# A hybrid decoder layer: weights split into high and low parts by whole loaded tiles instead of halves

## The chip, the core and the metric

The kernel runs on one core of a Trainium2 chip. The core has engines with instruction streams of their own: TensorE (PE, matrix products; its weight loads are listed as PEld), VectorE (DVE), ScalarE (ACT), GpSimd (POOL) and SyncE (SP), which issues most of the transfers. They wait for each other by semaphores. The metric is the device time of one execution in microseconds; a profile is one such execution, recorded instruction by instruction.

## What is computed

One layer over 256 tokens of width 2048, batch 1, all in float32. Cut to its skeleton, with the shapes written behind:

```
u    = rms_norm(x, norm1_g)                  # 256 x 2048
proj = u @ w_in                              # 2048 x 6432
q, k, v, z = split(proj)                     # 3 x 1024 columns, and 3360 for z
attn = dilated_attention(q, k, v, bias)      # 16 heads of 64, three dilation patterns
rw   = rwkv7_time_mix(z, ...)                # 16 heads of 64, a recurrence over the tokens
h    = x + concatenate(attn, rw) @ w_out     # 2048 x 2048
u    = rms_norm(h, norm2_g)
gate, up = split(u @ w_gate_up)              # 2048 x 11264
h    = h + (silu(gate) * up) @ w_down        # 5632 x 2048
return rms_norm(h, final_g)
```

Both sides of every large product are float32. The kernel writes a weight w as a sum of two parts in the matmul's own rounded float32 type (F32R): high, a rounded copy of w, and low, w minus that copy. The activation is split likewise. A product is then three matmuls: high times high, high activation times low weight, low activation times high weight.

## The kernel before

**The weights' way.** All large weights pass one pipeline, in the order of a list `plan`: first the 288 low-rank columns of z (called `lo`), then per half of the heads the columns of r, k, v (z) and of v, q, k (attention), then w_out, then gate and up in turn for 11 groups of 512 hidden columns, then w_down in four slabs of 512 output columns. An entry of `plan` is one load: 1024 columns of float32 on 128 partitions, which are two chunks (kc) of 128 rows by 512 columns, or four chunks of 128 by 256, or in `lo` two of 128 by 288. The stages:

- `load` (L121 on): SP issues a DMA (L126) from the weight into a raw tile `wr`. There are RAWB = 3 raw tiles.
- `make` (L134 to L151): for each half j of the raw tile ACT copies it into `wh` (L148, the rounded high part), and DVE subtracts that copy from the raw tile into `wl` (L149, the low part). A half is one chunk of 512 or two of 256. There are SPLB = 6 buffers of 512 columns for wh and as many for wl.
- `take` (L158 to L166): hands one chunk to a consumer, and calls `make` ahead, so that in the program's order some 6 chunks (AHEAD), that is three tiles, are split ahead of the one in use.
- consumers: `slab` (L169, six matmuls per chunk of 512, L178 to L180), `slab_T` (L183, chunks of 256, L191 to L193), `slab_2T` (L1062, eight matmuls per chunk for gate and up, L1068 and L1069).

The last 8 chunks of w_down (KEEP) are split into four tiles that stay, since each is read twice.

**What sets the order.** Beside the large products runs side work: the attention and the recurrence. Each piece of it is a generator, and `run` and `step` (L201 to L233) put steps of these generators between the chunks of the main products. The program text made so is then arranged by a scheduler into one fixed order for each engine. So a split stands in ACT's and DVE's rows between other work of these engines: a row that waits holds up what stands behind it. A raw tile is free for the next load when its last subtract is done; a wh or wl buffer is free when PE's last matmul on it is done.

**Names in the rows.** `u1h` is the high part of x transposed (made from `pt_u` by ACT, L252), `lo` the product of it with the 288 columns, `zlo` its scaled copy (L413, L416), which PE transposes (`ptlo`). `zkh`, `zrh`, `zvh` are products for one half of the heads, `z_zvh` and `zv_h` the steps that finish the last of these (L476, L344). `bsh` is a sum over heads made by two matmuls of `bhh` and `blh` (L553 to L557). `kp_h`, `y_h`, `mix`, `bk_h` are the recurrence's arrays on DVE. In the recurrence `Zh` is a product with the state `Sh` (L803), DVE adds it into `av_h` (L806), and PE turns that into `Xh` (L811). `p` and `o` are the products with w_out (`part`), `ga`, `gb`, `up` gate and up, `d` down.

Of the kernel before, what the change touches and what calls it, by code (L numbers as in the profile page):

```python
# [10 lines left out]
F32 = mybir.dt.float32  # L11
F32R = mybir.dt.float32r
AF = mybir.ActivationFunctionType
ALU = mybir.AluOpType
AX = mybir.AxisListType

P = 128
# [58 lines left out]
def layer(ctx: ExitStack, tc: tile.TileContext, I, out, dbg=None, upto=99):  # L76
    nc = tc.nc
    PE, ACT, DVE, POOL, SP = nc.tensor, nc.scalar, nc.vector, nc.gpsimd, nc.sync
# [6 lines left out]
    wp = ctx.enter_context(tc.tile_pool(name="wp", bufs=1))  # L85
# [31 lines left out]
    plan, made, wq = [], {}, [0, 0]  # L117
# [12 lines left out]
    def ahead(n):  # L130
        while len(raws) < min(n, len(plan)):
            load(len(raws))

    def make(i):  # L134
        w_ap, kcs, col, n, keep = plan[i]
        ahead(i + 1)
        raw = raws[i]
        g = 2 if n == 256 else 1
        for j in range(2):
            if keep:  # L140
                both = keep.pop(0)
                hi, lo = both[:, 0, :], both[:, 1, :]
            else:
                hi = wp.tile([P, 512], F32R, tag="whi", name=f"wh{i}_{j}", bufs=SPLB)
                lo = wp.tile([P, 512], F32R, tag="wlo", name=f"wl{i}_{j}", bufs=SPLB)
            hi, lo = (a.rearrange("p (g n) -> p g n", g=g) for a in (hi, lo))
            src = raw[:, j * g:(j + 1) * g, :n]
            ACT.activation(hi[:, :, :n], src, AF.Copy)  # L148
            DVE.tensor_tensor(lo[:, :, :n], src, hi[:, :, :n].bitcast(F32), op=ALU.subtract)  # L149
            for k in range(g):  # L150
                made[(w_ap.tensor.name, kcs[j * g + k], col)] = (hi[:, k, :], lo[:, k, :])  # L151

    def plan_slab(w_ap, kcs, col, n, keep=None):
        g = 4 if n == 256 else 2
# [3 lines left out]
    def take(w_ap, kc, col, units=1):  # L158
        key = (w_ap.tensor.name, kc, col)
        while wq[0] < len(plan) and (key not in made or wq[0] * 2 < wq[1] + AHEAD):  # L160
            make(wq[0])
            wq[0] += 1
        wq[1] += units
        return made.pop(key)
# [151 lines left out]
    for half in range(2):  # L316
        for blks in ((4, 3, 5), (2, 0, 1)):
            for blk in blks:
                col = blk * AW + half * 512
# [16 lines left out]
    keep = []  # L336
# [689 lines left out]
    fp = ctx.enter_context(tc.tile_pool(name="fp", bufs=1, reuse_waits="tile"))  # L1026
# [5 lines left out]
    u2 = [fp.tile([P, 4, 2, SEQ], F32R, tag=f"u2{g}", name=f"u2{g}") for g in range(4)]  # L1032
# [74 lines left out]
        POOL.dma_start(t, I["final_g"].rearrange("(o d) -> o d", o=1)[:, i * 1024:(i + 1) * 1024].broadcast_to([P, 1024]))  # L1107
    fg = lambda sl: fgs[sl // 2][:, sl % 2 * 512:sl % 2 * 512 + 512]
    for g in range(4):
        kt = fp.tile([P, 2, 2, 512], F32R, tag=f"u2{g}", name=f"kept{g}")  # L1110
        keep += [kt[:, 0], kt[:, 1]]
    outr = out.rearrange("o (t p) d -> p (o t) d", p=P)
    hlhs = pair(hid_h, hid_l)

# [41 lines left out]
        print("SBUF free", tile.free_sbuf_bytes_per_partition(tc))  # L1156


RAWB, SPLB, AHEAD = 3, 6, 6
KEEP = 8  # L1160
LAT = (6, 5, 2, 6, 5, 3)
BS = 1.0
# [28 lines left out]
```

## Time and profile before

| | |
|---|---|
| median of 3 runs | 1232.54 us (1231.67 to 1233.33) |
| the profiled execution | 1232.04 us, of it 1230.3 us are its span |
| PE busy | 1214.8 us |
| DVE busy | 818.4 us |
| ACT busy | 698.7 us |
| bytes moved by DMA | 224.05 MB |

How such rows are read. In a list of groups a row has the line, the engine, the operation, what is written and read with their shapes, the count, the busy time in us and the mean of one in ns, and behind the last bar how long the engine was idle just ahead of them, and what ended that. In a timeline a row has the start and the length in us; "x3" behind it means that three such instructions follow each other and are drawn as one, and the square bracket has the idle time ahead and what ended it. A list of waits has total, count and longest. The roughly 1.7 us between span and time lie outside the recorded instructions.

### The profile page before, as it was taken

The page shows a single profiled execution, that of the slowest core. Times are in us where ns is not written, and L with a number is a line of the kernel's source. Part 1 is how long each engine was busy: PE and PEld are TensorE (multiplying, and loading weights), DVE is VectorE, ACT ScalarE, POOL GpSimd, SP SyncE. Part 2 cuts the span into 40 slices and gives each one's busy share as a digit, 9 for nine tenths or more (in the row PEclk, how much of TensorE's full clock was granted, in tenths as well). Part 3 has the DMA queues.
Part 4 walks back from the last instruction along what each step waited for, and adds up shares of the span by engine and source line. Part 5 has one row for each costly group of instructions (what it writes and reads, how often), then busy time and mean ns, then how long its engine had stood idle before and what let it go on. Part 6 is the DMA issues. An engine that isn't in the chain of part 4 may idle for free.

```text
span 1230.3 us, 21227 instructions
## 1 busy us (share of the span) xinstructions
PE 1214.8 (99%) x7932; PEld 1061.2 (86%) x7932; DVE 818.4 (67%) x1561; ACT 698.7 (57%) x1328; POOL 39.5 (3%) x64
## 2 busy tenths in 40 slices
PE   8999999999999999999999999999999999999997
PEld 7998999898997788888888888888888888888885
DVE  5887786698787467666666666566566655555653
ACT  7874546584556556655555555555565555454443
POOL 4000000001000000000000000000000000010100
PEclk9999999999999999999999999999999999999999
DMA  8656566356566257666666666666666666666663
GB/s 249 201 160 193 154 178 173 85 151 178 168 192 183 86 167 227 189 199 193 189 189 189 189 190 188 191 189 193 193 188 193 189 189 190 199 192 194 184 202 139
DMA packets 148472, 224.05 MB, mean 182 GB/s; under 512 B 18396, under 2 KB 65760, under 8 KB 148368
## 3 DMA queue, kind: packets, MB, share of 16 engines
q1 hardware_dynamic: 132176, 211.12, 58.3%
q10 hardware_dynamic: 13920, 6.06, 1.9%
q0 software_dynamic: 2272, 5.50, 1.4%
q8 instruction: 62, 1.02, 0.4%
q14 instruction: 42, 0.34, 0.1%
HBM read 218.96 MB, written 3.69 MB: 181 GB/s over the span
## 4 chain that ended last, share of the span: by engine, by line
PE 93%; DVE 2%; DMA 2%; ACT 1%; issue 1%; SPq 0%; POOLq 0%; POOL 0%; ACTq 0%; DVEq 0%
PE up L1068 13%; PE gb L1068 7%; PE ga L1068 7%; PE up L1069 7%; PE d L179 6%; PE d L178 6%; PE d L180 6%; PE gb L1069 3%; PE ga L1069 3%; PE o L178 2%; PE o L180 2%; PE o L179 2%; PE kTb L191 1%; PE qTb L191 1%; PE kTb L192 1%; PE kTb L193 1%
## 5 line engine op out<-in xcount | busy, mean ns | idle before, releaser
L149 DVE TENSOR_TENSOR wl<-wr,wh 128x512 fp32r<-128x512 f32 (+1 forms) x792 | 541.7, 691 | 338.4 <-ACT wh L148 321.1
L148 ACT ACTIVATE wh<-wr 128x512 fp32r<-128x512 f32 (+1 forms) x792 | 493.3, 627 | 466.3 <-DVE wl L149 234.8
L1068 PE MATMUL up<-u,wh 128*128 128x512 f32 x704 | 244.6, 394 | 0.0
L1069 PE MATMUL up<-u,wl 128*128 128x256 f32 x704 | 195.0, 277 | 0.0
L1068 PEld LDWEIGHTS up<-u,wh 128*128 128x128 f32 x704 | 132.0, 188 | 30.7
L1069 PEld LDWEIGHTS up<-u,wl 128*128 128x128 f32 x704 | 132.1, 188 | 0.0
L178 PE MATMUL d<-wh,hh 128*128 128x512 f32 x336 | 130.7, 389 | 0.0
L180 PE MATMUL d<-wh,hl 128*128 128x512 f32 x336 | 130.7, 389 | 0.0
L179 PE MATMUL d<-wl,hh 128*128 128x512 f32 x336 | 130.7, 389 | 0.0
L1068 PE MATMUL gb<-u,wh 128*128 128x512 f32 x352 | 130.2, 394 | 0.0
L1068 PE MATMUL ga<-u,wh 128*128 128x512 f32 x352 | 130.0, 394 | 0.0
L1069 PE MATMUL ga<-u,wl 128*128 128x256 f32 x352 | 97.5, 277 | 0.0
L1069 PE MATMUL gb<-u,wl 128*128 128x256 f32 x352 | 97.5, 277 | 0.0
L1068 PEld LDWEIGHTS ga<-u,wh 128*128 128x128 f32 x352 | 66.0, 188 | 15.3
L1068 PEld LDWEIGHTS gb<-u,wh 128*128 128x128 f32 x352 | 66.0, 188 | 15.2
L178 PEld LDWEIGHTS d<-wh,hh 128*128 128x128 f32 x336 | 63.1, 188 | 13.2
L180 PEld LDWEIGHTS d<-wh,hl 128*128 128x128 f32 x336 | 63.1, 188 | 13.1
L179 PEld LDWEIGHTS d<-wl,hh 128*128 128x128 f32 x336 | 63.1, 188 | 13.0
L1069 PEld LDWEIGHTS ga<-u,wl 128*128 128x128 f32 x352 | 66.0, 188 | 0.1
L1069 PEld LDWEIGHTS gb<-u,wl 128*128 128x128 f32 x352 | 66.1, 188 | 0.0
L178 PE MATMUL o<-wh,mixh 128*128 128x512 f32 x96 | 38.3, 399 | 0.0
L179 PE MATMUL o<-wl,mixh 128*128 128x512 f32 x96 | 37.6, 392 | 0.0
(340 smaller groups left out, 2070.2 us busy)
## 6 DMA issues: line engine op xcount, KB each, us to landing
wr<-in_w_gate_up_dram SPq DMA_DIRECT2D x176, 512.0 KB, 4.3
wr<-in_w_in_dram SPq DMA_DIRECT2D x96, 512.0 KB, 3.8
wr<-in_w_down_dram SPq DMA_DIRECT2D x88, 512.0 KB, 4.4
wr<-in_w_out_dram SPq DMA_DIRECT2D x32, 512.0 KB, 4.7
wr<-in_w_in_dram SPq DMA_DIRECT2D x8, 288.0 KB, 4.9
x_sb<-in_x_dram SPq DMA_DIRECT2D x8, 256.0 KB, 6.8
biasa<-rvd ACTq DMA_DIRECT2D x4, 512.0 KB, 4.4
xs<-in_x_dram POOLq DMA_DIRECT2D x4, 512.0 KB, 5.7
```

Source lines behind the costliest of these rows:

```text
L148: ACT.activation(hi[:, :, :n], src, AF.Copy)
L149: DVE.tensor_tensor(lo[:, :, :n], src, hi[:, :, :n].bitcast(F32), op=ALU.subtract)
L178: PE.matmul(o, ah[:, sl], hi[:, :n], start=first, stop=False)
L179: PE.matmul(o, ah[:, sl], lo[:, :n], start=False, stop=False)
L180: PE.matmul(o, al[:, sl], hi[:, :n], start=False, stop=fin)
L191: PE.matmul(o, hi[:, cb], uh_, start=kc == 0, stop=False)
L192: PE.matmul(o, hi[:, cb], ul_, start=False, stop=False)
L193: PE.matmul(o, lo[:, cb], uh_, start=False, stop=kc == NK - 1)
L1068: PE.matmul(ps[b], hi[:, cb], u, start=kc == 0, stop=False)
L1069: PE.matmul(ps[b][:, 0:SEQ], lo[:, cb], u[:, 0, :], start=False, stop=kc == NK - 1)
```

## The change

`make` no longer goes over two halves. One ACT copy takes the whole raw tile into a `wh` of 1024 columns, and one DVE subtract makes a `wl` of 1024 columns (in `lo`, 2 x 288 of them). There are three such buffers of each, in the same space as the six before. The kept tiles become four of 2 x 1024 columns. The loads, the matmuls, `take` and AHEAD stay as they are. The lines behind `make` move up by two, those behind the kept tiles by three.

```diff
-        g = 2 if n == 256 else 1
-        for j in range(2):
-            if keep:
-                both = keep.pop(0)
-                hi, lo = both[:, 0, :], both[:, 1, :]
-            else:
-                hi = wp.tile([P, 512], F32R, tag="whi", name=f"wh{i}_{j}", bufs=SPLB)
-                lo = wp.tile([P, 512], F32R, tag="wlo", name=f"wl{i}_{j}", bufs=SPLB)
-            hi, lo = (a.rearrange("p (g n) -> p g n", g=g) for a in (hi, lo))
-            src = raw[:, j * g:(j + 1) * g, :n]
-            ACT.activation(hi[:, :, :n], src, AF.Copy)
-            DVE.tensor_tensor(lo[:, :, :n], src, hi[:, :, :n].bitcast(F32), op=ALU.subtract)
-            for k in range(g):
-                made[(w_ap.tensor.name, kcs[j * g + k], col)] = (hi[:, k, :], lo[:, k, :])
+        if keep:
+            both = keep.pop(0)
+            hi, lo = both[:, 0, :], both[:, 1, :]
+        else:
+            hi = wp.tile([P, 1024], F32R, tag="whi", name=f"wh{i}", bufs=SPLB)
+            lo = wp.tile([P, 1024], F32R, tag="wlo", name=f"wl{i}", bufs=SPLB)
+        hi, lo = (a.rearrange("p (g n) -> p g n", g=4 if n == 256 else 2) for a in (hi, lo))
+        src = raw[:, :, :n]
+        ACT.activation(hi[:, :, :n], src, AF.Copy)
+        DVE.tensor_tensor(lo[:, :, :n], src, hi[:, :, :n].bitcast(F32), op=ALU.subtract)
+        for k, kc in enumerate(kcs):
+            made[(w_ap.tensor.name, kc, col)] = (hi[:, k, :], lo[:, k, :])
...
-        kt = fp.tile([P, 2, 2, 512], F32R, tag=f"u2{g}", name=f"kept{g}")
-        keep += [kt[:, 0], kt[:, 1]]
+        keep.append(fp.tile([P, 2, 1024], F32R, tag=f"u2{g}", name=f"kept{g}"))
...
-RAWB, SPLB, AHEAD = 3, 6, 6
+RAWB, SPLB, AHEAD = 3, 3, 6
```

The scheduler arranges the engines' rows anew. Three places follow; the numbers behind the names are buffer numbers, which differ between the two programs.

At the start, on ACT, around the copies of the second half of x (`pt_u_10`, `pt_u_12`), before:

```order
L148 ACTIVATE wh_0_279<-wr_277 128x288
L148 ACTIVATE wh_1_283<-wr_277 128x288
L252 ACTIVATE u1h_90<-pt_u_10_324,par_75 128x256
L252 ACTIVATE u1h_91<-pt_u_12_377,par_75 128x256
L405 ACTIVATE sqj_449,acc<-x_sb 128x512
L405 ACTIVATE sqj_451,acc<-x_sb 128x512
L148 ACTIVATE wh_0_301<-wr_299 128x288
L148 ACTIVATE wh_1_305<-wr_299 128x288
L252 ACTIVATE u1h_90<-pt_u_10_324,par_75 128x256
```

The same place on ACT in the change:

```order
L146 ACTIVATE wh_259<-wr_257 128x2x288
L250 ACTIVATE u1h_90<-pt_u_10_296,par_75 128x256
L250 ACTIVATE u1h_91<-pt_u_14_350,par_75 128x256
L250 ACTIVATE u1h_91<-pt_u_12_341,par_75 128x256
L403 ACTIVATE sqj_405,acc<-x_sb 128x512
L146 ACTIVATE wh_277<-wr_275 128x2x288
```

The second `u1h_90` from `pt_u_10` stood behind both copies of a further tile (`wr_299`), and now stands ahead of that tile's copy (`wr_275`).

On DVE, where the first half of the heads is finished (at 284 us of the profile before), before:

```order
L862 SCALAR_TENSOR_TENSOR y_h_2974<-y_h_2974,par,kp_h_973 128x256 x3
L866 SCALAR_TENSOR_TENSOR mix_1377<-y_h_2974,par,mix_1377 128x256 x4
L149 TENSOR_TENSOR wl_1_3803<-wr_3796,wh_1_3802 128x512
L476 TENSOR_TENSOR z_zvh_3824<-zvh_0_3640,rbc_83 128x256
L476 TENSOR_TENSOR z_zvh_3828<-zvh_1_3641,rbc_83 128x256
L149 TENSOR_TENSOR wl_0_3843<-wr_3840,wh_0_3842 128x512
L344 SCALAR_TENSOR_TENSOR zv_h_3639<-z_zvh_3824,par,zv_h_3639 128x255
L344 SCALAR_TENSOR_TENSOR zv_h_3639<-z_zvh_3828,par,zv_h_3639 128x255
L149 TENSOR_TENSOR wl_1_3847<-wr_3840,wh_1_3846 128x512
```

The same place on DVE in the change:

```order
L860 SCALAR_TENSOR_TENSOR y_h_2714<-y_h_2714,par,kp_h_885 128x256 x3
L864 SCALAR_TENSOR_TENSOR mix_1253<-y_h_2714,par,mix_1253 128x256 x4
L474 TENSOR_TENSOR z_zvh_3508<-zvh_0_3340,rbc_83 128x256
L474 TENSOR_TENSOR z_zvh_3512<-zvh_1_3341,rbc_83 128x256
L147 TENSOR_TENSOR wl_3527<-wr_3524,wh_3526 128x1024
L342 SCALAR_TENSOR_TENSOR zv_h_3339<-z_zvh_3508,par,zv_h_3339 128x255
L342 SCALAR_TENSOR_TENSOR zv_h_3339<-z_zvh_3512,par,zv_h_3339 128x255
```

The second half of one tile (`wl_1_3803`) stood behind the `mix` rows; in the change that tile is split whole further up, and the next tile's split (`wl_3527`) is one row behind `z_zvh`, where its first half stood.

On PE, in the second half's recurrence, from the last `Zh` product to `Xh`, before:

```order
L803 MATMUL Zh_5555<-Sh_5517,arh_3609 64x64
L178 MATMUL o_0_5498<-wh_0_5400,mixh_4945 128x512
L179 MATMUL o_0_5498<-wl_0_5401,mixh_4945 128x512
L180 MATMUL o_0_5498<-wh_0_5400,mixl_4946 128x512
L178 MATMUL o_1_5499<-wh_0_5400,mixh_4945 128x512
L179 MATMUL o_1_5499<-wl_0_5401,mixh_4945 128x512
L180 MATMUL o_1_5499<-wh_0_5400,mixl_4946 128x512
L811 MATMUL Xh_5574<-av_h_4385,U_h_5044 64x64 x8
```

The same step on PE in the change:

```order
L801 MATMUL Zh_5091<-Sh_5057,arh_3309 64x64
L178 MATMUL o_0_5038<-wh_4948,mixl_4518 128x512
L176 MATMUL o_1_5039<-wh_4948,mixh_4517 128x512
L177 MATMUL o_1_5039<-wl_4949,mixh_4517 128x512
L809 MATMUL Xh_5110<-av_h_4009,U_h_4612 64x64
L178 MATMUL o_1_5039<-wh_4948,mixl_4518 128x512
L833 MATMUL Yh_5089<-arh_3309,Sh_5057 64x64
L809 MATMUL Xh_5110<-av_h_4009,U_h_4612 64x64 x7
```

Six matmuls of the product with w_out stood between the last `Zh` and `Xh`; in the change it is three, and one more comes behind the first `Xh`.

## Prediction

> **What bounds the kernel now.** The page comes first: the busy shares, then the chain that ended last.
>
> ```profile
> PE 1214.8 (99%) x7932; PEld 1061.2 (86%) x7932; DVE 818.4 (67%) x1561; ACT 698.7 (57%) x1328; POOL 39.5 (3%) x64
> PE 93%; DVE 2%; DMA 2%; ACT 1%; issue 1%; SPq 0%; POOLq 0%; POOL 0%; ACTq 0%; DVEq 0%
> ```
>
> PE works in 1214.8 of 1230.3 us, so the idle time that any change to the splits could remove is 15.5 us. The table by stage says where it lies (columns: window, its length, then busy time of PE, PEld, DVE, ACT, POOL, granted clock, DMA share, GB/s).
>
> ```profile
> 0.00:30.00 30.00, 25.64 (x148) 23.25 (x149) 17.62 (x48) 21.78 (x57) 14.34 (x31) 0.94 0.85 249
> 260.00:300.00 40.00, 38.86 (x273) 36.02 (x273) 38.20 (x80) 25.11 (x41) 3.16 (x6) 1.00 0.59 168
> 500.00:600.00 100.00, 100.00 (x580) 87.47 (x579) 62.04 (x112) 56.17 (x106) 0.00 (x0) 1.00 0.66 190
> 1200.00:1231.00 31.00, 21.61 (x96) 17.57 (x94) 11.85 (x23) 11.00 (x23) 1.10 (x2) 0.91 0.39 135
> ```
>
> The ends hold 4.4 and 9.4 us of idle PE. The last window's is the closing normalization and the stores, which the change doesn't touch. From 500 to 600, a stretch of gate/up like those behind it, PE has no gap at all, while DVE is 62% and ACT 56% busy. Only around 280 is DVE full (38.20 of 40). PE's list of waits names what is left:
>
> ```profile
> PE bsh L557 <- DVE blh L553: 2.1, 3, 1.0
> PE lo L178 <- ACT u1h L252: 1.9, 1, 1.9
> ```
>
> None is a wait for wh or wl. The splits are on the chain nowhere for long; the kernel is bound by PE's own matmuls, which the change neither removes nor shortens.
>
> **What the change removes.** 792 half splits become 396 whole ones, and the 8 kept halves 4 tiles.
>
> ```profile
> L149 DVE TENSOR_TENSOR wl<-wr,wh 128x512 fp32r<-128x512 f32 x776 | 535.3, 695 | 335.7 <-ACT wh L148 318.4 <-PE up L1068 6.9 <-PE ga L1068 6.9
> L148 ACT ACTIVATE wh<-wr 128x512 fp32r<-128x512 f32 x776 | 487.0, 631 | 461.9 <-DVE wl L149 234.8 <-PE gb L1068 39.8 <-PE up L1068 36.5
> L860 DVE TENSOR_TENSOR y_h<-y_h,sq_h 128x1024 f32<-128x1024 f32 x2 | 2.4, 1220 | 1.0 <-ACT sq_h L859 1.0
> L857 ACT ACTIVATE sq_h<-y_h 128x1024 f32<-128x1024 f32 x2 | 2.1, 1054 | 0.5 <-DVE y_h L854 0.5
> ```
>
> The trace has no split of 1024, but it has 1024-wide instructions of both engines: I price a whole tile at 1.05 us on ACT and 1.22 on DVE. Against two halves (2 x 0.631, 2 x 0.695) 388 tiles save 388 x 0.21 = 81 us of ACT's busy time and 388 x 0.17 = 66 us of DVE's. On the path this is worth nothing by itself, since PE covers both. What can change the time is when a split is ready. A first half is now ready only when the whole tile is: ACT's copy takes 0.42 longer (1.05 - 0.63) and DVE's subtract 0.53 longer (1.22 - 0.69), so about 0.95 us later from the same start. And a buffer is given back after two chunks, not one.
>
> **Gate/up and down (500 to 1216 us).** One tile in steady state:
>
> ```profile
> 599.43 0.63 ACT L148 ACTIVATE wh<-wr 128x512 fp32r<-128x512 f32 x1 [0.76 <-DVE wl L149]
> 600.09 0.69 DVE L149 TENSOR_TENSOR wl<-wr,wh 128x512 fp32r<-128x512 f32 x1 [0.69 <-ACT wh L148]
> 601.48 0.69 DVE L149 TENSOR_TENSOR wl<-wr,wh 128x512 fp32r<-128x512 f32 x1 [0.69 <-ACT wh L148]
> wr<-in_w_gate_up_dram SPq DMA_DIRECT2D x176, 512.0 KB, 4.3
> ```
>
> Halves follow every 1.39 us (601.48 - 600.09), so a tile lasts PE 2.78. With three whole buffers, PE's last matmul on one frees it for the tile three further on, which is needed two tiles later, after 5.56 us. ACT and DVE need 1.05 + 1.22 plus about 0.1 of handing over: ready after 2.4, spare 3.1. The raw tile is free after the same 2.4, its load lands 4.3 later, at 6.7, and ACT's copy of it is due at 8.3 (three tiles): spare 1.6. The tightest place in the trace is a slab's end at which ACT had a table load and four activations ahead of the copies:
>
> ```profile
> 521.46 1.90 DVE L149 TENSOR_TENSOR wl<-wr,wh 128x512 fp32r<-128x512 f32 x3 [1.83 <-ACT wh L148]
> 524.70 0.27 PE L1069 MATMUL up<-u,wl 128*128 128x256 f32 x1
> ```
>
> The first of the three, a second half, ends at 522.15; PE first reads that tile's wl at 524.70, 2.55 later. Less 0.95 leaves 1.6. Term: 0. The cover is the three tiles of lead; without it each tile would cost up to 0.95 us.
>
> DVE's two halves back to back take about 1.29 us in this trace, not 1.39, so of the 0.17 us saved a tile only 0.07 is throughput where DVE is full. The Trainium skill, "Perfetto Trace Analysis", section on optimizing Scalar/DVE operations, says that a larger instruction helps an engine that is saturated, and that breaking instructions up can help where the engine isn't saturated but makes bubbles on others. By the first half of that rule DVE's window around 280 gains; by the second this change could only harm the rest, with PE at 99%. The sum below would be the same by both.
>
> **The start (0 to 30 us).** Here are the loads that come late, and PE's largest wait inside the work.
>
> ```profile
> L149 DVE TENSOR_TENSOR wl<-wr,wh 128x288 fp32r<-128x288 f32 x16 | 6.5, 451 | 2.7 <-ACT wh L148 2.7
> L148 ACT ACTIVATE wh<-wr 128x288 fp32r<-128x288 f32 x16 | 6.2, 441 | 4.5 <-DMA wr<-in_w_in_dram 4.4
> 22.45 0.46 ACT L252 ACTIVATE u1h<-pt_u,par 128x256 fp32r<-128x256 f32 x1
> 22.96 0.40 PE L178 MATMUL lo<-wh,u1h 128*128 128x288 f32 x1 [1.91 <-ACT u1h L252]
> 24.00:27.40 3.40, 3.40 (x17) 3.40 (x16) 3.21 (x11) 3.22 (x8) 1.82 (x3) 0.50 0.89 252
> ```
>
> ACT makes u1h of chunk 10 behind two copies of a tile whose load was late, and PE stands still for 1.91 us; then the clock is 0.50 for 3.4 us. In the new order the u1h stands ahead of that tile's copy, so the 1.9 goes. What is late next: a whole split of 2x288 frees its raw tile later than its first half did, by up to one half's 0.45; each load behind it follows as much later, and with it the last products of `lo` and the zlo copies, which stand on ACT behind the whole copy of a further tile and for whose transposes PE waits. Bounds: gain 1.9 and the half-rate window's lost half (1.7), or lose one more such window (1.7). I take **0**, the middle: the loads that this stretch needs are the same, its DMA share is 0.89 to begin with, so a wait that goes is likely to return at the next load.
>
> The Trainium skill, "TensorE: Matmul & The Clock Gate", section on the HAM clock gate, has half clock follow an idle window of about 3.4 us (4096 cycles) that runs freely. The row has the length, 3.4 us at 0.50, but after only 1.9 us of idle. By the page a wait under 3.4 us would cost no clock, and the upper end would be its wait alone.
>
> **Where DVE is full (280 to 292 us).**
>
> ```profile
> 283.35 1.67 DVE L866 SCALAR_TENSOR_TENSOR mix<-y_h,par,mix 128x256 f32<-128x256 f32 x4
> 284.93 0.69 DVE L149 TENSOR_TENSOR wl<-wr,wh 128x512 fp32r<-128x512 f32 x1
> 285.53 0.75 DVE L476 TENSOR_TENSOR z_zvh<-zvh,rbc 128x256 f32<-128x256 f32 x2
> 286.20 0.68 DVE L149 TENSOR_TENSOR wl<-wr,wh 128x512 fp32r<-128x512 f32 x1
> 286.80 0.88 DVE L344 SCALAR_TENSOR_TENSOR zv_h<-z_zvh,par,zv_h 128x255 f32<-128x255 f32 x2
> 287.09 0.28 PE L193 MATMUL zvh<-u1h,wl 128*128 128x256 f32 x1
> 265.40 0.50 PE L557 MATMUL bsh<-blh,onesblk 128*128 128x512 f32 x1 [0.89 <-DVE blh L553]
> 293.23 0.50 PE L557 MATMUL bsh<-blh,onesblk 128*128 128x512 f32 x1 [0.25 <-DVE blh L553]
> ```
>
> A half split ends at 286.88 and PE reads it at 287.09: 0.2 us of lead, the smallest behind the start. Now the tile before is split whole ahead of the mix instructions, so 284.93's half is gone from here, and the whole split of the next tile stands behind z_zvh. Working: the earlier half moved forward delays mix by 1.22 - 0.69 = 0.53; without the 0.6 of the half at 284.93, z_zvh ends about 286.1 (286.20 + 0.53 - 0.6), and the split at 287.1 to 287.6, against 287.09: stall 0 to 0.5. Term: **+0.4**. The bsh waits (2.1 in three) go by DVE's queue: the one at 265.40 shrinks by some 0.2 (blh stands behind fewer, longer splits there), the one of 0.25 at 293.23 goes since PE gets more to do ahead of it, and the third stays. Term: **-0.4**, bounds 0 and -2.1.
>
> **Interruptions and the recurrence.** The order of PE differs; it leaves a run of projection matmuls for a side matmul 331 times, not 325. The price of one is in these rows:
>
> ```profile
> 370.74 0.39 PE L180 MATMUL p<-wh,mixl 128*128 128x512 f32 x1
> 371.06 0.93 PE L908 MATMUL Sa<-kTb,qTb 64*128 64x128 f32 x8
> 371.91 0.50 PE L178 MATMUL p<-wh,mixh 128*128 128x512 f32 x1
> ```
>
> The side matmul starts 0.32 behind the projection matmul, where two projection matmuls in one run are 0.23 apart (412.70 - 412.47 below): 0.09 each, and six are **+0.5**. The way back isn't priced; it may cost as much again. In the second half's recurrence the matmuls between Z and X shrink from six to three:
>
> ```profile
> 410.82 0.68 PE L803 MATMUL Zh<-Sh,arh 64*64 64x64 f32 x16
> 412.20 0.74 DVE L806 TENSOR_TENSOR av_h<-Zh,av_h 64x256 f32<-64x256 f32 x2
> 412.47 0.39 PE L179 MATMUL p<-wl,mixh 128*128 128x512 f32 x1
> 412.70 0.39 PE L180 MATMUL p<-wh,mixl 128*128 128x512 f32 x1
> 413.02 1.14 PE L811 MATMUL Xh<-av_h,U_h 64*64 64x64 f32 x16
> ```
>
> Six matmuls of 0.23 cover 1.4 us between Z's end and X, three cover 0.7; av_h's first addition needs about 0.4 of it (half of 0.74 and the handing over) if DVE is free. A whole split in front of it (1.22) makes PE wait about 1 us. Free: 0.15 each, in two or three steps; blocked: up to 1 each. In the new order no split stands right ahead of these av_h, so I take the free end, **+0.5**, bounds 0.3 and 2.
>
> **Sum.** 0 + 0 + 0.4 - 0.4 + 0.5 + 0.5 = +1.0 us against the profiled execution, which took 1232.04 (its span 1230.3 and 1.7 around it): 1233.0. The median of the runs is 1232.54, 0.5 above that execution, so the forecast for a median is **1233.5**.
>
> **The rivals.** *Faster, because waits go.* The 1.9 us for u1h, the half-rate window behind it (1.7) and both bsh terms (1.0) leave without a successor: 1.9 + 1.7 + 1.0 = 4.6, against the 0.4 at 287: 1232.5 - 4.2 = 1228.3. For it speaks that the order of ACT does remove the wait; against it the late loads. *Slower, because a first half waits for its whole tile.* One mechanism: DVE's 1.22 us split sits in front of a short instruction, or of a tile's first use, in the stretch from 30 to 500 us, where side work shares DVE. It decides when the lead (0.2 at 287) is under 0.95, or the cover of Z to X (0.7) is under the split plus 0.4. At one place a wait of 0.5 to 1.0; at five or six it is +4: about 1237.5. Against it speaks that PE's list has no wait for a split now, and that even 0.95 us less leaves 1.6 us at the worst place of gate/up. *The start turns the wrong way:* the loads, some 0.45 later for each of the four tiles behind the first, cost 1.7 (4 x 0.45 is 1.8), and one more window at half clock 1.7: +3.4, so 1233.5 + 3.4 = 1236.9.
>
> That the splits don't become whole is no rival: the engines' orders hold them.
>
> **How the numbers follow.** A measurement of this kernel can tell about 0.2% (2.5 us) from no change: under 1230.1 is faster, above 1235.0 slower. Forecast with its small terms 0.63, faster rival 0.13, slower splits 0.14, wrong start 0.10. Faster **0.13**, same **0.63**, slower **0.24**. The range runs from the faster rival's upper part, 1230.0, to 1237.0, the middle of the two slower ones; of these 0.12 is left out above and some 0.07 below.
>
> **What would show it.** Right: by-form rows of 1024 at 1.05 and 1.22 us; DVE some 66 and ACT some 81 us less busy; PE 100% in every window from 500 to 1200 with the pitch unchanged; no PE wait for wl but at 284 to 288; no 1.9 wait for u1h; Z to X with waits under 0.2. Wrong: a PE wait for wl or wh in gate/up or down, a granted clock under 1.00 past 30 us, splits dearer than 1.3 us, or a PE busy time that moves by more than a microsecond.

## The result, and the profile after

The changed kernel took 1245.07 us (median of 4 runs, 1243.05 to 1248.8) against 1232.54 before; the ratio is 1.0096, with a 95% interval of 1.0079 to 1.0113. By the prediction's bound of 0.2% it is slower, by 12 us, and outside the forecast's range. The profiled execution took 1244.41 us, 12.4 more than the one before, and its span is 1242.6.

The head of the page after (busy times, then the chain):

```profile
PE 1224.9 (99%) x7932; PEld 1065.0 (86%) x7932; DVE 775.1 (62%) x1161; ACT 628.7 (51%) x928; POOL 39.2 (3%) x64
PE 82%; issue 7%; DMA 4%; DVE 4%; ACT 3%; SPq 0%; POOLq 0%; POOL 0%; DVEq 0%; ACTq 0%
```

The first thing to see is that PE is busy 10.1 us longer (1224.9 against 1214.8) **with the same 7932 matmuls**. It isn't idle more; its matmuls take longer. The groups by shape say which: first two lines of before, then the same two of after and a group of the down product.

```profile
L1068 PE MATMUL up<-u,wh 128*128 128x512 f32 x704 | 244.6, 394 | 0.0
L1069 PE MATMUL up<-u,wl 128*128 128x256 f32 x704 | 195.0, 277 | 0.0
```

```profile
L1066 PE MATMUL up<-u,wh 128*128 128x512 f32 x704 | 249.5, 399 | 0.0
L1067 PE MATMUL up<-u,wl 128*128 128x256 f32 x704 | 197.7, 281 | 0.0
L176 PE MATMUL d<-wh,hh 128*128 128x512 f32 x336 | 130.7, 389 | 0.0
```

The matmuls of gate and up are longer by 4 to 5 ns in the mean, and those of down are what they were (389 on the page before). The stages, with the first window's row of before ahead:

```profile
600.00:700.00 100.00, 100.00 (x579) 87.45 (x578) 64.72 (x121) 57.45 (x113) 0.00 (x0) 1.00 0.66 190
```

```profile
500.00:515.00 15.00, 15.00 (x88) 13.20 (x88) 7.24 (x9) 6.20 (x6) 0.00 (x0) 1.00 0.68 198
600.00:700.00 100.00, 100.00 (x568) 86.66 (x567) 58.27 (x77) 47.45 (x69) 0.00 (x0) 1.00 0.64 188
```

Count the matmuls in brackets behind PE's time: 568 in 100 us after, 579 before, at a granted clock of 1.00 and a PE without a gap in both. That is a pace 1.94% slower (579/568). Over gate and up behind their first slab (516 to 982 us before, 466 us) it makes 9.0 us. The first gate slab, 500 to 515, still has 88 in both kernels, though its splits are whole too. So something happens between the first gate slab and the first up slab. PE's timeline of after at that place:

```profile
520.02 0.39 PE L1066 MATMUL up<-u,wh 128*128 128x512 f32 x1
520.25 0.27 PE L1067 MATMUL up<-u,wl 128*128 128x256 f32 x1
520.47 0.50 PE L1066 MATMUL up<-u,wh 128*128 128x512 f32 x1
520.81 0.28 PE L1067 MATMUL up<-u,wl 128*128 128x256 f32 x1
```

A matmul on wh starts 0.11 or 0.12 us behind the one on wl ahead of it; here it is 0.22. PE paused for 0.11 us, and the matmul behind the late one starts 0.34 behind it, not 0.23, so some 0.21 us are lost here in all. The page counts no idle time, since the modelled end of the matmul ahead covers it; only the list of waits of the weight loads names it. ACT's timeline says why:

```profile
PEld up L1066 <- ACT rbc L261: 0.3, 1, 0.3
```

```profile
519.10 1.06 ACT L146 ACTIVATE wh<-wr 128x1024 fp32r<-128x1024 f32 x1
520.07 0.35 ACT L261 COPY rbc<-rbc 128x256 f32<-128x256 f32 x1
```

The fourth bank of the up product is the one that held `rbc`; it is free when ACT has copied `rbc` out, and that copy stood behind a whole split of 1.06 us: it ended at 520.42, and the product started 0.05 later. Before, it stood behind a half and one short copy, ended at 516.99, and the product wanted the bank at 517.18 (the copy, then the product):

```profile
516.60 0.39 ACT L263 COPY rbc<-rbc 128x256 f32<-128x256 f32 x1
517.18 0.40 PE L1068 MATMUL up<-u,wh 128*128 128x512 f32 x1
```

Counted from the first product that makes `rbc` (515.70 before, 518.88 after), the copy starts 0.90 us behind it before and 1.19 after, 0.29 later.

The rest of the 12.4 us lies ahead of gate: its first matmul starts at 495.62, and at 492.59 before.

```profile
492.59 0.39 PE L1068 MATMUL ga<-u,wh 128*128 128x512 f32 x1
981.95 0.28 PE L1069 MATMUL up<-u,wl 128*128 128x256 f32 x1
```

```profile
495.62 0.39 PE L1066 MATMUL ga<-u,wh 128*128 128x512 f32 x1
994.27 0.28 PE L1067 MATMUL up<-u,wl 128*128 128x256 f32 x1
```

So in these two executions 3.0 us come ahead of gate, gate and up together take 498.65 instead of 489.36 (**+9.3**), and behind them nothing is lost (12.3 late at 994.27, 12.3 or 12.4 at the end).

### The profile page after: what moved, and what is told of

Read it like the earlier page. It is cut to its first block, busy times and chain, and to the rows that moved or that the text cites. A ratio compares the mean times of both kernels' runs of the same rounds, so it can differ in the third digit from the quotient of the medians.

```text
span 1242.6 us, 19871 instructions
## 1 busy us (share of the span) xinstructions
PE 1224.9 (99%) x7932; PEld 1065.0 (86%) x7932; DVE 775.1 (62%) x1161; ACT 628.7 (51%) x928; POOL 39.2 (3%) x64
## 4 chain that ended last, share of the span: by engine, by line
PE 82%; issue 7%; DMA 4%; DVE 4%; ACT 3%; SPq 0%; POOLq 0%; POOL 0%; DVEq 0%; ACTq 0%
PE up L1066 13%; PE up L1067 7%; PE gb L1066 7%; PE ga L1066 7%; PE d L177 6%; PE d L178 6%; PE d L176 6%; PE gb L1067 3%; PE ga L1067 3%; DVE wl L147 2%; DMA wr<-in_w_in_dram 1%; PE qTb L189 1%; PE qTb L191 1%; PE qTb L190 1%; PE vb L176 1%
## 5 line engine op out<-in xcount | busy, mean ns | idle before, releaser
L147 DVE TENSOR_TENSOR wl<-wr,wh 128x1024 fp32r<-128x1024 f32 (+1 forms) x396 | 482.6, 1220 | 377.9 <-ACT wh L146 376.6
L146 ACT ACTIVATE wh<-wr 128x1024 fp32r<-128x1024 f32 (+1 forms) x396 | 416.4, 1052 | 510.4 <-PE d L178 125.4
L1066 PE MATMUL up<-u,wh 128*128 128x512 f32 x704 | 249.5, 399 | 0.0
L1067 PE MATMUL up<-u,wl 128*128 128x256 f32 x704 | 197.7, 281 | 0.0
L178 PE MATMUL o<-wh,mixl 128*128 128x512 f32 x96 | 37.9, 397 | 0.0
```

The lines of the kernel that those rows point to most:

```text
L178: PE.matmul(o, al[:, sl], hi[:, :n], start=False, stop=fin)
L1066: PE.matmul(ps[b], hi[:, cb], u, start=kc == 0, stop=False)
L1067: PE.matmul(ps[b][:, 0:SEQ], lo[:, cb], u[:, 0, :], start=False, stop=kc == NK - 1)
```

## The experiments

Two theories stood against each other. **A**: a pause of PE, however short, can leave its loads and matmuls in another rhythm, which stays until the next pause. **B**: the wide instructions of ACT and DVE slow the matmuls beside them. Ten kernels were run. A chunk is 8 matmuls of gate or up; its time below is the mean distance of chunk starts in the profiled execution behind the first up slab. The pause is how much later than usual the waiting product starts.

| run | splits | pause of PE in the first up slab | chunk, us | profiled execution | all runs, us |
|---|---|---|---|---|---|
| before | halves | none | 1.387 | 1232.04 | 1230.9 to 1234.95, and 1238.2, 1238.5 (53 runs) |
| the change | whole | 0.11 | 1.413 | 1244.41 | 1243.05 to 1248.8 (4) |
| e1 | whole | none | 1.387 | 1234.54 | 1232.73 to 1235.02 (10) |
| e2 | halves | 0.13 | 1.387 | 1231.98 | 1231.64 to 1236.16 (8), 1240.75, 1242.43 |
| e3 | halves | 0.19 | 1.387 | 1234.26 | 1234.26, and 1241.61 to 1247.03 (6) |
| e9 | halves | 0.25 | 1.413 | 1239.8 | 1239.8 to 1242.13 (4) |
| e5 | whole | 0.15 | 1.387 | 1234.91 | 1234.29 to 1235.01 (4), 1238.93, 1239.14, 1242.48 to 1243.89 (3) |
| e10 | whole | 0.24 | 1.413 | 1244.26 | 1244.01 to 1247.27 (4) |
| e6 | whole | 0.30 | 1.413 | 1243.77 | 1237.32, 1242.79 to 1244.98 (3) |
| e4 | whole | 0.11, and held up again at 745 | 1.413 | 1243.05 | 1243.05 to 1244.57 (4) |
| e7 | whole from gate on | none | 1.387 | 1238.69 | 1238.69 to 1241.57 (5) |
| e8 | halves | none | 1.387 | 1232.97 | 1232.08 to 1234.26 (11) |

**e1: the copy of rbc on DVE.** One instruction of the change is moved:

```diff
-        ACT.copy(dst, pr[:, 0:SEQ])
+        (DVE.tensor_copy if pool is fp_[0] else ACT.copy)(dst, pr[:, 0:SEQ])
```

> The changed kernel, with one instruction moved: the copy of rbc out of PSUM between the first gate slab and the first up slab is made by DVE, not by ACT, where it stood behind a whole copy of 1.06 us. In the trace of the change PE waits there for 0.22 us (start 520.47), and from there on every chunk of gate/up takes 1.410 to 1.421 us, not 1.387, to the end of gate/up; the gate slab ahead of the wait, with whole tiles too, had 1.387. Theory A (a pause leaves PE's loads and matmuls in another rhythm, which stays until the next pause): no pause, chunks of 1.387 throughout, 338 x 0.027 = 9 us less, 1236.0 (1235.3 to 1236.8). Theory B (the wide instructions of ACT and DVE slow the matmuls while they run): the pace stays at 1.41, 1245 (1243 to 1249).

1234.33 us, ratio to before 1.0008 (0.9998 to 1.0017). The splits are as whole as in the change, and the pace is that of before:

```profile
518.85 0.42 DVE L263 COPY rbc<-rbc 128x256 f32<-128x256 f32 x1
```

```profile
600.00:700.00 100.00, 100.00 (x579) 87.44 (x578) 60.90 (x84) 50.05 (x75) 0.00 (x0) 1.00 0.60 190
```

The copy (first row, DVE's timeline) now starts at 518.85, well ahead of the bank's next use, and the window has 579 matmuls again. Theory B falls: wide splits run beside every one of them. It came out a microsecond below A's range: I had left the change's full 3.0 us ahead of gate in the sum, and here gate starts at 494.97, not at 495.62. Against the runs of before beside it (median 1233.44) 0.9 are left.

**e2, e3 and e9: before, with a pause made on purpose.** In the kernel before, with half splits, ACT reads the rbc bank one, two or three times more, into a buffer that nothing reads (a name `rbc_` holds this rbc, so that the other call is left alone):

```diff
         ACT.copy(dst, pr[:, 0:SEQ])
+        if dst is rbc_[0]:
+            for e in range(2):
+                ACT.copy(late, pr[:, 0:SEQ])
```

> The kernel before, splits in halves, with one more ACT copy that reads the rbc bank again behind its first copy (into a buffer that nothing reads). The bank then comes free about 0.27 us later, at some 517.26 of the profile before, and the up product that uses this bank next wants it at 517.07 to 517.18: a pause of PE of 0.1 to 0.2 us. Theory A: the pace of gate/up falls to 1.41 a chunk with no wide split in the program, 1241.5 (1240.5 to 1243), unless the pause happens to end in the same rhythm (then 1232.7). Theory B: 1232.7 (1232 to 1233.5), chunks of 1.387.

> The same with two such extra reads, so that the bank comes free about 0.54 us later and PE pauses for 0.4 us. Theory A: the rhythm that follows depends on where the pause ends: 1242 if slow, 1233 if the old one; the run shows whether every pause does it. Theory B: 1233.0, chunks of 1.387.

> The kernel before with three extra reads of the rbc bank (a pause of PE of some 0.6 to 0.7 us), splits in halves. A1 (the rhythm after a pause is drawn by the moment at which it ends, whatever the splits' width): runs at 1233 and at 1242 both possible, the profile shows 1.387 or 1.410 to 1.421 a chunk behind the pause and its time fits. If only the pause of 0.4 us of the run with two reads led there: all runs at 1233.5.

Medians 1233.64 (ratio 0.999 to 1.0033), 1242.09 (1.004 to 1.0091) and 1241.8 (1.0051 to 1.0081). With one extra read eight of ten runs stay near before and two are at 1241 and 1242; with two and three all but one are 7 to 14 us longer. That one, 1234.26, is the profiled one of e3. A profile is one execution: that of e9 caught the long rhythm, with no wide split in the program (below: PE's timeline at the pause, the window, the group).

```profile
516.20 0.27 PE L1075 MATMUL up<-u,wl 128*128 128x256 f32 x1
516.56 0.50 PE L1074 MATMUL up<-u,wh 128*128 128x512 f32 x1
```

```profile
600.00:700.00 100.00, 100.00 (x568) 86.70 (x567) 63.72 (x119) 56.66 (x111) 0.00 (x0) 1.00 0.65 188
```

```profile
L1074 PE MATMUL up<-u,wh 128*128 128x512 f32 x704 | 249.5, 399 | 0.1
```

The distance at the pause is 0.36 instead of 0.11, and behind it stand the change's own numbers: 568 matmuls in 100 us, 249.5 us for the group. The profile of e3 has the long rhythm elsewhere: its first gate slab runs at 1.413 a chunk, and behind the small work between gate and up it has 1.387. The pause did not end it. Already ahead of the pause, the matmuls on wl start 233, 231 and 232 ns behind those on wh, where the long rhythm has one of 240 or 241 in every three; so the long rhythm had ended at the small work, and the pause of 0.19 didn't bring it back.

With one read the pause was as expected (0.13), with two and three it was shorter (0.19 and 0.25, against 0.4 and 0.6 to 0.7). The product that waits isn't the same one: with one read it is the fourth on wh behind the small work, as in the change, with two the fifth, with three the sixth. I read this as the scheduler putting products of the next chunk ahead of the waiting one; the rows don't name the bank.

**e4: the small work once more.** In the change the two products for rbc and their copy are done again between gate and up of group 5:

```diff
-        if f == 0:
+        if f in (0, 5):
```

> The changed kernel with the same small work between gate and up (two products for rbc and ACT's copy of them) done once more, between gate and up of group 5 (its result is the same as the first). It puts a second break into PE's row in the middle of gate/up. Theory A: the pace can change at that place and nowhere else: 1241 if it returns to 1.387 there (about 185 chunks left x 0.027 = 5 less), 1245.5 if it stays slow, another value if a third rhythm exists. Theory B: 1245.5, 1.41 on both sides.

1243.67 us (1.0071 to 1.0101). The chunks have 1.413 on both sides of the second piece of work:

```profile
600.00:700.00 100.00, 100.00 (x568) 86.74 (x567) 58.96 (x81) 49.01 (x73) 0.00 (x0) 1.00 0.59 186
800.00:900.00 100.00, 100.00 (x567) 86.76 (x567) 57.64 (x76) 47.10 (x68) 0.00 (x0) 1.00 0.59 187
```

But the second piece held PE up again, at the same product and for the same copy. The list of the weight loads' waits counts two, and the product at 745.31, though it starts on time, has the next one 0.34 behind it instead of 0.23:

```profile
PEld up L1066 <- ACT rbc L261: 0.4, 2, 0.3
```

```profile
745.31 0.50 PE L1066 MATMUL up<-u,wh 128*128 128x512 f32 x1
745.65 0.28 PE L1067 MATMUL up<-u,wl 128*128 128x256 f32 x1
```

So e4 doesn't tell whether the rhythm lasted through the small work or was ended by it, as in e3, and begun again by a hold-up of 0.11 us.

**e5, e10 and e6: the change, with a longer pause.** The same one, two and three extra reads, in the changed kernel.

> The changed kernel with one extra ACT read of the rbc bank, so that PE's pause between gate and up of the first group is some 0.27 us longer (about 0.5). Theory A1 (the rhythm is drawn anew at each pause, by the exact moment at which it ends): runs of 1236 and of 1245 both occur, the profile's pace fits its own span. Theory A2 (with whole tiles in the program any pause there ends in the slow rhythm): all runs 1243 to 1249.

> The changed kernel with two extra reads (a pause between those of one and of three, some 0.8 us). A1: a mixture of 1235 and 1244, perhaps with values between; the profile says what a run between them has.

> The same with three extra reads, a pause of about 1.2 us. A1: again both kinds of runs, in other shares; A2: all runs 1244 to 1250.

Medians 1238.93 (1.0025 to 1.0065), 1244.49 (1.0081 to 1.0115) and 1243.28 (1.0051 to 1.0098). As they were stated, A1 holds against A2: in e5 four of nine executions are at 1234 to 1235 and three at 1242 to 1244, and the profiled one (1234.91) has the pace of before, with whole splits and with a pause. But e5 isn't the change with a longer pause alone. Two matmuls on wh follow each other at the pause, which they do there in no other of these kernels:

```profile
519.22 0.89 PE L1072 MATMUL up<-u,wh 128*128 128x512 f32 x2
```

The second of them starts 0.38 us behind the first, where 0.23 is usual, so the pause is 0.15. With whole splits and PE's products in the usual order (the change, e4, e10, e6) every profile has the long rhythm; the one shorter run of e6, 1237.32, wasn't profiled. For these A2 isn't ruled out. The pauses, 0.15 to 0.30 us, were again much shorter than expected, and again at another product (the sixth in e10, the seventh in e6).

**e7 and e8: whole splits only from gate on; the copy on DVE before.** e7 takes e1 and splits the tiles ahead of gate by halves again, in buffers of whole tiles:

```diff
-        ACT.activation(hi[:, :, :n], src, AF.Copy)
-        DVE.tensor_tensor(lo[:, :, :n], src, hi[:, :, :n].bitcast(F32), op=ALU.subtract)
+        gg = 4 if n == 256 else 2
+        parts = [slice(0, gg // 2), slice(gg // 2, gg)] if i < 136 else [slice(0, gg)]
+        for p_ in parts:
+            ACT.activation(hi[:, p_, :n], src[:, p_], AF.Copy)
+            DVE.tensor_tensor(lo[:, p_, :n], src[:, p_], hi[:, p_, :n].bitcast(F32), op=ALU.subtract)
```

> Whole splits only from the first gate tile on (gate, up, down), half splits in buffers of whole tiles ahead of it, and the rbc copy on DVE, so that no pause follows in gate/up. If the rest of the change's cost (1 us of the run with rbc on DVE alone) lies in the stretch ahead of gate, as the forecast's terms said: 1233.4, no difference from before. If it lies in gate, up and down: 1234.3.

> The kernel before with only the rbc copy moved to DVE. Theory A: PE's chance pauses at that place go, and with them the single runs of 1238 that the kernel before shows; the median stays at 1233 (1232.5 to 1233.5), and the highest run is under 1236. If those runs have another cause, they are there too.

e7 missed: 1240.51 (1.0045 to 1.0071). Its gate and up have 579 matmuls in 100 us, so nothing is lost there, but gate starts only at 499.05. Halves in buffers of whole tiles aren't the kernel before: the engines' rows were arranged anew, and PE waits at new places ahead of gate.

```profile
PE lo L179 <- ACT u1h L253: 1.9, 1, 1.9
PE bsh L559 <- ACT bhh L555: 1.7, 1, 1.7
PE pt_u L248 <- DVE h_sb L1052: 1.7, 1, 1.7
```

It shows that whole splits from gate on cost gate and up nothing, and leaves open which part of the change makes the 2 to 3 us ahead of gate. e8 is 1232.87 (0.9991 to 1.001), no faster than before; its highest of 11 runs is 1234.26, but the runs of 1238 are so rare before (2 of 53) that their absence there shows little.

No version beats the kernel before. The change without its cost is e1, which is equal to before within the measurement.

## Why the prediction was wrong

- **The step that failed** is the one on gate/up and down: "Term: 0", with its "cover is the three tiles of lead". It asked only whether a *split* comes late for PE, and none does. It didn't ask what else stands behind the longer instructions on ACT. There is one such thing at 520: a copy that frees a PSUM bank, 0.29 us later behind its product, and PE is late by 0.11 us. The 0.11 us itself would have been lost among the terms; what it led to, 9.3 us, was in none of them. e1 takes the late copy away and gets the time back, and e9 gets the same pace with half splits.
- The step behind it: "PE 100% in every window from 500 to 1200 with the pitch unchanged". The 100% held and the pitch didn't. I took PE's pace at given shapes and clock as a constant of the kernel. It has two values here. The prediction's own sign for this came: PE's busy time moved by more than a microsecond, by 10.1.
- The slower rival named the right kind of thing (a long split in front of a short instruction, 30 to 500 us, DVE), at 1237.5 and with a price of one wait. The place was in gate/up, the engine ACT, and the price wasn't that of the wait. The rule that the prediction drew from the Trainium skill, "Perfetto Trace Analysis", section on optimizing Scalar/DVE operations, that breaking instructions up can help where an engine isn't saturated but makes bubbles on others, agrees with the row at 520.07: ACT was 51% busy, and its whole split made the bubble of 0.11 us.
- Durations: by-form rows of after.

```profile
L147 DVE TENSOR_TENSOR wl<-wr,wh 128x1024 fp32r<-128x1024 f32 x388 | 476.6, 1229 | 375.0 <-ACT wh L146 373.8
L146 ACT ACTIVATE wh<-wr 128x1024 fp32r<-128x1024 f32 x388 | 410.8, 1060 | 506.2 <-PE d L178 125.4 <-PE gb L1066 105.8 <-PE up L1066 99.0
```

  1.22 and 1.05 us were forecast, 1.23 and 1.06 measured: right. By these groups 59 us of DVE and 76 of ACT were saved (535.3 - 476.6, 487.0 - 410.8), a little under the 66 and 81 forecast; the engines' whole busy times fell by 43.3 and 70.0 (818.4 to 775.1, 698.7 to 628.7). As the prediction said, none of it shows in the time.
- The start, term 0: the wait of 1.9 for u1h went, in all six profiles with the change's rows there. Waits of 1.0 for zlo and 0.6 for wl came in its place, and at 187 us, at the first product `Sa`, the two profiles are 0.25 apart (187.14 and 187.39). The expectation that a wait which goes returns at the next load held: ACT's copy ahead of that zlo waited 1.2 for its load. The window at half clock went too (the row from 0 to 30 has a granted clock of 1.00, and 0.94 before), but that is no sure gain. With the same rows in the start, e9 has no such window among the kernels with halves and e2 has one at 8 us instead of 24; of the six with whole splits, three (e1, e5, e10) have one of 3.4 us at 8 us, and 0.94 too. So whether the 1.7 is paid depends on the execution as well.

```profile
0.00:30.00 30.00, 26.75 (x158) 23.30 (x159) 18.08 (x40) 21.74 (x50) 14.89 (x31) 1.00 0.82 245
```

```profile
PE bsh L555 <- DVE blh L551: 1.7, 3, 0.9
PE up_wh L500 <- DVE up_w L306: 1.3, 1, 1.3
PE PTa L932 <- DVE sa L924: 1.0, 1, 1.0
PE ptlo L444 <- ACT zlo L411: 1.0, 1, 1.0
PE lo L177 <- DVE wl L147: 0.6, 2, 0.4
```

- The stretch to gate, forecast +1.0 with the start: the profile after has +3.0, e1's 1234.33 against 1233.44 is +0.9 in the median of runs. One profile against one says little here. Ahead of gate, before, e2, e3, e8 and e9 have the same rows, and gate starts at 491.04 to 494.14 (mean 492.7); the change, e1, e4, e5, e6 and e10 have the same rows too, and it starts at 493.80 to 495.62 (mean 494.9). That is +2.1 in the mean. Of the terms, the bsh waits fell by 0.4 in sum as forecast (2.1 to 1.7), but by luck: the one of 0.25 at 293.23 went as forecast, but one of 0.32 came at 298.81, the one at 265.40 stayed (0.89, then 0.88), and the third, which was to stay, fell from 0.97 to 0.53. No PE wait shows between 284 and 291, so the +0.4 there was too much. No wait ahead of an Xh is over 0.1, as forecast; what the interruptions cost isn't measured. Two waits that I had not priced came, 1.3 for up_w and 0.8 more for sa.

**What stays open.** What in PE makes two rhythms isn't settled. In the profiled executions the short rhythm repeats after four pairs of matmuls (1.387 us, 0.347 a pair; in e3 every pair is alike, at the same pace) and the long one after three (1.060, 0.353), whatever the tiles. By the times of the runs, the pause's length doesn't decide alone: 0.11 us led to the long one in all eight runs of the change and e4, 0.13 in two of ten, 0.15 in some, 0.19 in six of seven, 0.24 and 0.25 in all eight. Nor does the splits' width: e9 has the long one with halves. But the pauses were measured in one execution of each kernel, they aren't all at the same product, and the change and e2, which wait at the same product for nearly the same time, mostly went opposite ways. Whether whole splits make the long rhythm likelier after a pause isn't shown. The runs between the two levels (1237 to 1239) weren't caught in a profile.

## What to carry to other kernels

When PE is busy 99% of the time and a change makes it slower, compare its busy time at equal counts of matmuls before looking for waits: a longer mean at the same shape and clock is a pace, not a wait, and a count of matmuls per window shows where it begins. Before making an instruction longer, list all that stands behind it on its engine, above all short copies that free a PSUM bank, not only its own consumers. In e1 it was enough to give such a copy to the other engine, where it came earlier.

## What the hardware showed that I had not expected

PE's pace for one and the same row of matmuls has two stable values, 1.387 and 1.413 us a chunk, at a granted clock of 1.00. It can change at a pause of a tenth of a microsecond and then holds for over 460 us, through the slab boundaries; in e3 the long one ended at the small work between gate and up. The down product, with 512 columns in every matmul, has one value in all profiles, 389 to 390 ns in the mean. Such a pause turned a difference of 0.1 us into 9, and in the kernel before, an extra copy of 0.27 us that nothing needs made the kernel 0.65% slower in the median when it was done twice.
